# Expert weight loads held behind the first gathered rows, and a cross-attention output product in halves

## The chip, the cores and the metric

The kernel runs on one core of one Trainium2 chip. The metric is the device time of one execution in microseconds (us). The core has five engines that run their own queues: PE (matrix products), DVE (vector work), ACT (activations and copies), POOL, which here issues the indirect transfers, and SP, which issues most plain transfers. All transfers run on the core's 16 DMA engines. PE's granted clock stands in the profile as a share of full speed.

## The reference

Two transformer blocks in float32 on 512 tokens of width 1024. The change touches only the end of the second block: cross attention to a memory of 256 rows, and after it a mixture of 16 experts, of which each token uses two.

```python
x = x + cross_attention(rmsnorm(x, norm_xa_g), rmsnorm(mem, norm_mem_g), xa_wq, xa_wk, xa_wv, xa_wo)
x = x + hierarchical_moe(rmsnorm(x, norm_moe_g), ...)
return rmsnorm(x, norm_final_g)

def hierarchical_moe(h, ...):
    ...                                   # group softmax, best group, top 2 of its 4 experts
    a = jnp.einsum("nd,edf->nef", hf, w_gate)      # 1024 -> 256 per expert
    b = jnp.einsum("nd,edf->nef", hf, w_up)
    u = jax.nn.silu(a) * b * combine[..., None]    # combine: routing weights, zero for experts not chosen
    return jnp.einsum("nef,efd->nd", u, w_down)    # 256 -> 1024
```

## The kernel before

Tokens stand in four tiles of 128 rows (`self.x[t]`, two halves of 512 columns). Products keep float32 precision by splitting each operand into a high and a low part: `wsplit` makes the high part on ACT (a copy) and the low part on DVE (a subtraction), and each product is three matmuls (`mm_as`, lines L380 to L382). So every weight tile costs a load (`wl`, 512 KB), an ACT and a DVE instruction (`ws`, L354 and L357) before PE can use it.

**The end of cross attention.** `cross_out(t)` multiplies the attention output of tile t by `w_xo` in two halves n and adds each to `x` (L1420). `route_unit(t)` then routes the tile: transposes of `x` (L1466), the logits (L1480, L1482), the choice of experts on DVE (L1484 to L1499), the rank of each token within its expert (L1506, L1509), and the normed rows `hr` (L1501), which SP writes to DRAM as `rows_d` (L1502). When tile 3 is through, `slot_ids` (L1551, L1552) gives for each expert the list `ids` of up to 96 rows. `weigh` (L1540 to L1545) puts the routing weights into the same slots: 8 products on PE and 16 small DVE instructions.

**The experts.** `expert(i)` gathers the rows of expert i by an indirect transfer of POOL (`gat`, L1667), transposes them on PE (L1674), splits them (`eh`, L423, L424), multiplies by the gate and up weights (24 matmuls, `wg` from four `wl` tiles), and later multiplies by the down weights (`wed`, four tiles of 256 KB; L1720 for the second half). POOL adds the result into DRAM (`acc_d`, L1726). A pipeline of generators (`pipe`) starts a new expert in each round; expert 16 is one that takes what overflows the 96 slots, and its weights are chosen by a register (L1628).

**The loads.** `fetch_all` is one list of steps, in order of experts: one step for each `wl` tile of the gate and up weights, and one for the four `wed` tiles of an expert, two experts behind. The cross attention takes the first `PF2` steps while it runs; then each round of the expert stage takes `NF` = 4 more. All are issued by SP, in order, and each waits until its buffer is free (the pool `p` holds the `wl` tiles, the pool `u` the `wed` tiles) and until the eighth transfer before it has landed. `rows_d` stands in the same queue, so it is issued between weight loads. With 18 steps, all of the gate and up weights of experts 0 to 3 and the down weights of experts 0 and 1 are asked for during cross attention; expert 4 follows in the first round.

The program's order on each engine is set by a scheduler that runs before the kernel is built; the lists below are taken from the built programs.

Of the kernel before, what the change touches and what calls it, by code (L numbers as in the profile page):

```python
# [22 lines left out]
NT = 4  # L23
# [9 lines left out]
FD, NF = 2, 4  # L33
# [21 lines left out]
CAP = 96  # L55
NX = 2 * S // CAP
HEADS = (slice(0, 64), slice(64, 128))
LAG = (1, 1, 1, 1)
PF0, PF1, PF2 = 2, 1, 18


def f32(ap):
# [3 lines left out]
def fl(t):  # L66
    return t.rearrange("p a b -> p (a b)")
# [111 lines left out]
def run(gen):  # L179
    for _ in gen:  # L180
        pass


def chain(*gens):
    for g in gens:
        yield from g


def pipe(gens, width, newest=False):

    act, gens = [], iter(gens)
    while True:
        if len(act) < width:
            g = next(gens, None)
            if g is not None:
                act.append(g)
        if not act:
            return
        for g in act[::-1] if newest else list(act):
            if next(g, g) is g:  # L200
                act.remove(g)
        yield


def take(gen, n):
    for _ in range(n):
        if next(gen, gen) is gen:
            return
        yield
# [15 lines left out]
class Block:  # L225
# [18 lines left out]
    def open(self, ctx):  # L244
        self.xp = self.sb(ctx, "xp")
        self.wk = self.sb(ctx, "work")
        self.n = N1
        self.nsplit, self.stage = -1, 0
        nc, ins = self.nc, self.ins
        self.x = [self.xt("x") for _ in range(NT)]  # L250
        self.load_x(0, 2)
        nc.sync.dma_start(self.ident, ins["ident"])
        nc.sync.dma_start(self.vec, ins["vec"])
        self.w_lora = [self.load(ins["w_lora"][:, g:g + 2, :], 160) for g in range(0, KD, 2)]
        self.load_x(2, 4)
# [88 lines left out]

    def load(self, src, n=512, tag="r"):
        t = self.pt("wl", F32, tag)[:, :src.shape[1], :n]
        self.nc.sync.dma_start(t, src)
        return t

    def wsplit(self, t, tags="hl"):  # L350

        nc = self.nc
        hi, lo = (self.pt("ws", F32R, g)[:, :t.shape[1], :t.shape[2]] for g in tags)
        nc.scalar.activation(hi, t, AF.Copy)  # L354
        self.nsplit += 1
        eng = nc.gpsimd if self.nsplit % 4 in SP[self.stage] else nc.vector
        eng.tensor_tensor(lo, t, f32(hi), ALU.subtract)  # L357
        return [(hi[:, j], lo[:, j]) for j in range(t.shape[1])]
# [16 lines left out]
    def mm_as(self, ps, ws, act, t, m=128):  # L375
        nt = self.nc.tensor
        sl = slice(t * m, (t + 1) * m)
        for k, (wh, wl) in enumerate(ws):
            ah, al = act[k]
            nt.matmul(ps, ah[:, sl], wh, start=k == 0, stop=False)  # L380
            nt.matmul(ps, ah[:, sl], wl, start=False, stop=False)  # L381
            nt.matmul(ps, al[:, sl], wh, start=False, stop=k == len(ws) - 1)  # L382

    def proj(self, src, act, use, rest=None, ws=None):

# [1026 lines left out]
    def cross_out(self, t, wo, z):  # L1412
        yield
        yield
        a = [(z[:, 0, h * 128:(h + 1) * 128], z[:, 1, h * 128:(h + 1) * 128]) for h in range(4)]
        for n in range(2):
            ps = self.ps("mm")
            self.mm_as(ps, wo[n], a, 0)
            x = self.x[t][:, n]
            self.nc.vector.tensor_tensor(x, x, ps, ALU.add)  # L1420
        yield


# [215 lines left out]
    def fetch_down(self, i):  # L1639

        w = []
        for ed in self.ed[i]:
            for k in range(2):
                w.append(self.ut("wed"))
                self.nc.sync.dma_start(w[-1], ed[:, k])
        self.ed[i] = w
        yield

# [7 lines left out]
    def expert(self, i, add=True, skip=dict(bounds_check=S - 1, oob_is_err=False)):  # L1656

        nc = self.nc

        def lag(n):  # L1660
            for _ in range(LAG[n]):
                yield

        raw = self.ew.pop(i)
        g = fl(self.xt("gat"))[:CAP]

        nc.gpsimd.indirect_dma_start(out=g, out_offset=None, in_=self.rows, **skip,  # L1667
                                     in_offset=bass.IndirectOffsetOnAxis(ap=self.ids[:CAP, i:i + 1], axis=0))
        yield from lag(3)
        a = []  # L1670
        for q in range(2):
            ps = self.ps("tp")[:, :4 * CAP]
            for k in range(4):
                nc.tensor.transpose(ps[:, k * CAP:(k + 1) * CAP], g[:, (4 * q + k) * 128:(4 * q + k + 1) * 128],  # L1674
                                    self.ident[:CAP, :CAP])
            z = self.pt("eh", F32R)
            h, l = (z[:, n, :4 * CAP] for n in range(2))
            self.split_to(h, l, ps)
            a += [(h[:, k * CAP:(k + 1) * CAP], l[:, k * CAP:(k + 1) * CAP]) for k in range(4)]
        self.stage = 6  # L1680
        with ExitStack() as c:

            for ins in self.last_of if i < 2 else ():
                c.enter_context(self.tc.issue_after(ins.ins))
            wg = [w for t in raw for w in self.wsplit(t)]
        yield from lag(0)
        ps = self.ps("mm")[:CAP]
        self.mm_as(ps, wg, a, 0, CAP)
        u = self.at("eu")[:CAP, :256]
        nc.scalar.activation(u, ps[:, :256], AF.Silu)  # L1690
        nc.vector.scalar_tensor_tensor(u, u, self.ws[:CAP, i:i + 1], ps[:, 256:], ALU.mult, ALU.mult)
        yield from lag(1)

        ed = self.ed.pop(i)
        hi, lo = self.pt("wdh", F32R, "r"), self.pt("wdl", F32R, "r")
        for k in range(2):
            self.split_to(hi[:, k], lo[:, k], ed[k])
        wd = [(hi[:, k], lo[:, k]) for k in range(2)]
        tp = self.ps("tp")
        for k in range(2):  # L1700
            nc.tensor.transpose(tp[:, k * CAP:(k + 1) * CAP], u[:, k * 128:(k + 1) * 128], self.ident[:CAP, :CAP])
        z, zf = self.tg("euT", "a", F32R), self.at("euF")
        self.split_to(z[:, :2 * CAP], z[:, 256:256 + 2 * CAP], tp[:, :2 * CAP])
        nc.scalar.copy(zf[:, :2 * CAP], tp[:, :2 * CAP])
        a = [(z[:, k * CAP:(k + 1) * CAP], z[:, 256 + k * CAP:256 + (k + 1) * CAP]) for k in range(2)]
        yield from lag(2)
        if add:
            y = self.kt("ey")[:CAP]
        else:
            oh = self.tg("oh", "u", F32R)[:CAP]  # L1710
            self.onehot(oh, i)
            yh, yl = (self.pt("yl", F32R)[:CAP] for _ in range(2))
            self.last += [(oh, yh), (oh, yl)]
        for n in range(2):
            ps = self.ps("mm")[:CAP]
            if n == 0:
                self.mm_as(ps, wd, a, 0, CAP)
            else:
                for k in range(2):
                    nc.tensor.matmul(ps, zf[:, k * CAP:(k + 1) * CAP], ed[2 + k], start=k == 0, stop=k == 1)  # L1720
            if not add:
                self.split_to(yh[:, n], yl[:, n], ps)
            else:
                nc.scalar.copy(y[:, n], ps)
        if add:
            nc.gpsimd.indirect_dma_start(  # L1726
                out=self.acc, out_offset=bass.IndirectOffsetOnAxis(ap=self.ids[:CAP, i:i + 1], axis=0),
                in_=fl(y), in_offset=None, compute_op=ALU.add)
        yield

    def moe(self, out):
        with ExitStack() as c:
            self.psum(c, "moe", mm=4, tp=3, r=1)
            p = pipe((self.expert(i, i < LAST) for i in range(17)), 16)
            ps, self.last = self.ps("r"), []
            self.route_weights()
            more = chain(self.weigh(self.ws[:CAP, 0:16], ps[:CAP, 0:16], self.rk, self.asg, 16), self.route_more())
            for n, _ in enumerate(p):
                run(take(self.fetches, NF))
                for _ in range(6 if n == 0 else 2):  # L1740
                    next(more, None)
                if n == GB:
                    gb = self.bcast_row(3)
            xs = [self.xt("fx") for _ in range(NT)]
            hs = [self.pt("fh") for _ in range(NT)]
            self.final(out, gb, xs, hs, self.last)
# [100 lines left out]
```

## Time and profile before

| | us |
|---|---|
| median of 3 runs | 1454.07 |
| range of the runs | 1453.44 to 1454.4 |
| the profiled execution, its own time | 1445.03 |
| its span in the trace | 1443.2 |
| PE busy | 1370.2 (95%) |
| DVE busy | 875.6 (61%) |
| ACT busy | 623.8 (43%) |
| POOL busy | 51.3 (4%) |
| mean granted clock of PE | 0.974 |

The profile is of one execution, 9 us shorter than the median of the runs. Its times are counted from the first instruction. Cross attention ends near 1226 us, the routing of the last tile takes until 1240 us, and the expert stage with the final norm fills the rest. The profile also says what each instruction waited for, in brackets behind its row.

### The profile page before, as it was taken

To read this page: it belongs to the slowest core of one execution; us is meant where nothing else is said; L and a number is where in the kernel's file an instruction comes from. 1 tells how busy PE (TensorE), PEld (TensorE's weight loads), DVE (VectorE), ACT (ScalarE), POOL (GpSimd) and SP (SyncE) were. 2 spreads that over 40 slices of the span, in tenths; PEclk is the share of its full clock that TensorE was granted. 3 is DMA by queue.
4 is the path that set the end of the run, shared out by engine and by line. 5 is a ranking of instruction groups with operands and counts; after the bars stand their busy time and mean duration, and the time that the engine had idled before them with its cause. 6 is when DMAs were issued, how large, how long until landed. Compare 5 with 4: busy or idle time off the path is not lost.

```text
span 1443.2 us, 21699 instructions
## 1 busy us (share of the span) xinstructions
PE 1370.2 (95%) x8366; PEld 1080.2 (75%) x8366; DVE 875.6 (61%) x2035; ACT 623.8 (43%) x1143; POOL 51.3 (4%) x45
## 2 busy tenths in 40 slices
PE   5999999998889999999999999999999998699996
PEld 5877776776588888888888887776788897466663
DVE  5347465646775145343367485997456566799875
ACT  5244235533334243232344414444432453487873
POOL 0000000000000000000000000000000000232211
PEclk9999999999899999999999999999999999699998
DMA  5322420121223233232242315222122345799984
GB/s 204 104 79 71 157 75 15 38 91 52 64 84 99 76 117 102 74 117 96 80 146 88 99 29 171 84 62 85 59 92 87 123 169 190 240 311 338 334 286 144
DMA packets 67759, 178.01 MB, mean 123 GB/s; under 512 B 17144, under 2 KB 18552, under 8 KB 67648
## 3 DMA queue, kind: packets, MB, share of 16 engines
q1 hardware_dynamic: 58676, 156.39, 32.7%
q0 software_dynamic: 3584, 10.10, 3.2%
q10 hardware_dynamic: 5388, 10.06, 2.0%
q8 instruction: 68, 1.11, 0.3%
q14 instruction: 43, 0.35, 0.1%
HBM read 163.12 MB, written 15.88 MB: 124 GB/s over the span
## 4 chain that ended last, share of the span: by engine, by line
PE 82%; DVE 10%; DMA 3%; ACT 2%; issue 2%; SPq 0%; DVEq 0%; ACTq 0%
PE mm L371 11%; PE mm L372 11%; PE mm L373 11%; PE mm L380 10%; PE mm L382 10%; PE mm L381 10%; PE q L966 3%; DVE ws L357 2%; PE mm L1720 2%; PE acc L537 1%; PE s L512 1%; PE tp L531 1%; DVE cacc L1112 1%; PE tp L917 1%; PE mm L917 1%
## 5 line engine op out<-in xcount | busy, mean ns | idle before, releaser
L357 DVE TENSOR_TENSOR ws<-wl,ws 128x1024 fp32r<-128x1024 f32 (+2 forms) x238 | 280.7, 1192 | 141.2 <-ACT ws L354 134.6
L354 ACT ACTIVATE ws<-wl 128x1024 fp32r<-128x1024 f32 (+2 forms) x238 | 244.3, 1034 | 176.3 <-PE mm L382 106.5
L371 PE MATMUL mm<-hT,ws 128*128 128x512 f32 (+3 forms) x872 | 314.7, 365 | 1.7 <-ACT qT L565 0.7
L372 PE MATMUL mm<-hT,ws 128*128 128x512 f32 (+3 forms) x872 | 314.4, 363 | 1.1 <-DVE hT L427 1.0
L373 PE MATMUL mm<-hT,ws 128*128 128x512 f32 (+3 forms) x872 | 313.0, 361 | 0.0
L371 PEld LDWEIGHTS mm<-hT,ws 128*128 128x128 f32 (+2 forms) x872 | 162.4, 188 | 30.1 <-ACT qT L565 1.4
L372 PEld LDWEIGHTS mm<-hT,ws 128*128 128x128 f32 (+2 forms) x872 | 163.2, 188 | 27.2 <-DVE hT L427 2.1
L373 PEld LDWEIGHTS mm<-hT,ws 128*128 128x128 f32 (+2 forms) x872 | 163.0, 187 | 24.9 <-DVE ws L357 0.2
L380 PE MATMUL mm<-ws,ff 128*128 128x512 f32 x256 | 100.0, 391 | 0.0
L382 PE MATMUL mm<-ws,ff 128*128 128x512 f32 x256 | 99.7, 389 | 0.0
L381 PE MATMUL mm<-ws,ff 128*128 128x512 f32 x256 | 99.6, 389 | 0.0
L1112 DVE SCALAR_TENSOR_TENSOR cacc<-sig,vec,cacc 128x507 f32<-128x507 f32 (+25 forms) x120 | 86.1, 733 | 1.6
L1067 DVE TENSOR_TENSOR ur<-ur 128x512 f32<-128x512 f32 x32 | 22.1, 692 | 82.3 <-ACT ff L1066 82.3
L380 PE MATMUL mm<-ws,eh 128*96 128x512 f32 x136 | 56.4, 415 | 1.1 <-ACT eh L423 1.1
L1063 ACT ACTIVATE ur<-mm 128x512 f32<-128x512 f32 x32 | 19.0, 594 | 87.1 <-PE mm L373 87.1
L382 PE MATMUL mm<-ws,eh 128*96 128x512 f32 x136 | 55.5, 408 | 0.7 <-DVE eh L424 0.6
L381 PEld LDWEIGHTS mm<-ws,ff 128*128 128x128 f32 x256 | 48.1, 188 | 9.9
L382 PEld LDWEIGHTS mm<-ws,ff 128*128 128x128 f32 x256 | 48.1, 188 | 10.0
L380 PEld LDWEIGHTS mm<-ws,ff 128*128 128x128 f32 x256 | 48.1, 188 | 9.9
L381 PE MATMUL mm<-ws,eh 128*96 128x512 f32 x136 | 54.7, 402 | 0.0
L521 ACT ACTIVATE sp<-sp,mx 128x128 f32<-128x128 f32 (+3 forms) x64 | 35.7, 558 | 30.2 <-DVE mx L519 30.1
L1086 DVE TENSOR_TENSOR f<-f,mm 128x512 f32<-128x512 f32 x24 | 16.4, 685 | 49.2 <-PE mm L382 49.2
(436 smaller groups left out, 2364.1 us busy)
## 6 DMA issues: line engine op xcount, KB each, us to landing
wl<-w_gu SPq DMA_DIRECT2D x68, 512.0 KB
wl<-w_p SPq DMA_DIRECT2D x60, 512.0 KB
wed<-w_ed SPq DMA_DIRECT2D x68, 256.0 KB
wl<-w_up SPq DMA_DIRECT2D x32, 512.0 KB
wl<-w_dn SPq DMA_DIRECT2D x32, 512.0 KB
wl<-w_out SPq DMA_DIRECT2D x16, 512.0 KB
x<-x SPq DMA_DIRECT2D x8, 512.0 KB
gram_d<-gb SPq DMA_DIRECT2D x8, 256.0 KB
```

The source lines that it names most:

```text
L354: nc.scalar.activation(hi, t, AF.Copy)
L357: eng.tensor_tensor(lo, t, f32(hi), ALU.subtract)
L371: nt.matmul(ps, wh[:, c0:c0 + m], ah[:, sl], start=k == 0, stop=False)
L372: nt.matmul(ps, wh[:, c0:c0 + m], al[:, sl], start=False, stop=False)
L373: nt.matmul(ps, wl[:, c0:c0 + m], ah[:, sl], start=False, stop=k == len(ws) - 1)
L380: nt.matmul(ps, ah[:, sl], wh, start=k == 0, stop=False)
L381: nt.matmul(ps, ah[:, sl], wl, start=False, stop=False)
L382: nt.matmul(ps, al[:, sl], wh, start=False, stop=k == len(ws) - 1)
L521: nc.scalar.activation(sps[h][:, :n], sps[h][:, :n], AF.Exp, scale=-1.0, bias=mxs[h][:, 0:1], accum_out=ls[h])
L917: nc.tensor.matmul(ps[a, c], lhs[a, c], rhs(a, c), start=True, stop=True)
L966: nc.tensor.matmul(ps[a], lhs[a], rhs[a], start=n == 0, stop=n == len(terms) - 1)
L1112: nc.vector.scalar_tensor_tensor(acc[:, d:], up[:, 0:S - d], w(30 - d), acc[:, d:], ALU.mult, ALU.add)
```

## The change

1. `PF2` goes from 18 to 13: cross attention asks for the weights of experts 0 to 2 and the down weights of expert 0 only. The 5 steps left out are taken in the first round of the expert stage, with the 4 of that round.
2. The loads of that round get a real wait (`hold`) for the gather of expert 0: they are issued when its rows have landed. SP's queue is in order, so all later loads follow them.
3. `cross_out` of tile 3 yields between its two halves, so that tile 2's routing can come between them.
4. The transposes of expert 1 are put behind the last gate product of expert 0 on PE; two of the four weight tiles of expert 0 may be split before the routing is over.
5. `weigh` moves from the first round to behind the gate products of expert 0, and `route_more` (the overflow plan) starts two rounds later.

```diff
-PF0, PF1, PF2 = 2, 1, 18
+PF0, PF1, PF2 = 2, 1, 13
...
         t = self.pt("wl", F32, tag)[:, :src.shape[1], :n]
-        self.nc.sync.dma_start(t, src)
+        self.hold(self.nc.sync.dma_start(t, src))
         return t
+
+    def hold(self, dma):
+
+        if self.behind is not None:
+            self.tc.add_manual_dep(dma.ins, self.behind.ins.name,
+                                   mybir.DependencyInfo(mybir.DependencyClass.Sync, mybir.DependencyReason.DATA),
+                                   reason="hold")
...
             self.mm_as(ps, wo[n], a, 0)
             x = self.x[t][:, n]
             self.nc.vector.tensor_tensor(x, x, ps, ALU.add)
+            if n == 0 and t == NT - 1:
+                yield
         yield
...
-        nc.gpsimd.indirect_dma_start(out=g, out_offset=None, in_=self.rows, **skip,
+        ga = nc.gpsimd.indirect_dma_start(out=g, out_offset=None, in_=self.rows, **skip,
                                      in_offset=bass.IndirectOffsetOnAxis(ap=self.ids[:CAP, i:i + 1], axis=0))
+        if i == 0:
+            self.behind = ga
         yield from lag(3)
...
-            for k in range(4):
-                nc.tensor.transpose(ps[:, k * CAP:(k + 1) * CAP], g[:, (4 * q + k) * 128:(4 * q + k + 1) * 128],
-                                    self.ident[:CAP, :CAP])
+            with ExitStack() as c:
+                if i == 1:
+                    c.enter_context(self.tc.issue_after(self.last_of[2].ins))
+                for k in range(4):
+                    nc.tensor.transpose(ps[:, k * CAP:(k + 1) * CAP], g[:, (4 * q + k) * 128:(4 * q + k + 1) * 128],
+                                        self.ident[:CAP, :CAP])
...
+            wg = [w for t in raw[:2] for w in self.wsplit(t)] if i == 0 else []
             for ins in self.last_of if i < 2 else ():
                 c.enter_context(self.tc.issue_after(ins.ins))
-            wg = [w for t in raw for w in self.wsplit(t)]
+            wg += [w for t in raw[len(wg) // 2:] for w in self.wsplit(t)]
         yield from lag(0)
         ps = self.ps("mm")[:CAP]
-        self.mm_as(ps, wg, a, 0, CAP)
+        last = self.mm_as(ps, wg, a, 0, CAP)
+        if i == 0:
+            self.last_of.append(last)
+            run(self.weights)
...
-            more = chain(self.weigh(self.ws[:CAP, 0:16], ps[:CAP, 0:16], self.rk, self.asg, 16), self.route_more())
+            self.weights = self.weigh(self.ws[:CAP, 0:16], ps[:CAP, 0:16], self.rk, self.asg, 16)
+            more = self.route_more()
             for n, _ in enumerate(p):
-                run(take(self.fetches, NF))
-                for _ in range(6 if n == 0 else 2):
+                run(take(self.fetches, NF + (5 if n == 0 else 0)))
+                self.behind = None
+                for _ in range(2 if n > 1 else 0):
                     next(more, None)
```

**SP's queue at the end of the routing.** Rows are instructions in program order, with the semaphores they wait for; DMAHW is the landing of one of SP's or ACT's own transfers, DMASW that of one of POOL's. In the program before, from the last load of expert 3 through the rows of tiles 1, 2 and 3:

```order
L347 DMA wl<-w_gu 128x1024 [waits DMAHW7_49,PE_49]
L1502 DMA rows_d<-hr 128x1024 [waits DMAHW0_49,DVE_49]
L1645 DMA wed<-w_ed 128x512 [waits DMAHW1_49,PE_49]
L1645 DMA wed<-w_ed 128x512 [waits DMAHW2_49,PE_49]
...
L1502 DMA rows_d<-hr 128x1024 [waits DMAHW7_49,DVE_49]
L347 DMA wl<-w_gu 128x1024 [waits DVE_49,DMAHW0_49,PE_49,Activation_49]
L1502 DMA rows_d<-hr 128x1024 [waits DMAHW1_49,DVE_49]
L347 DMA wl<-w_gu 128x1024 [waits DMAHW7_49,DMAHW2_49]
```

And with the change, from the rows of tile 1 on:

```order
L1512 DMA rows_d<-hr 128x1024 [waits DMAHW4_49,DVE_49]
L1512 DMA rows_d<-hr 128x1024 [waits DMAHW6_49,DVE_49]
L1512 DMA rows_d<-hr 128x1024 [waits DMAHW0_49,DVE_49]
L347 DMA wl<-w_gu 128x1024 [waits DMASW0_49,DMAHW1_49,PE_49,Activation_49]
L347 DMA wl<-w_gu 128x1024 [waits DMAHW4_49,DMAHW2_49]
L347 DMA wl<-w_gu 128x1024 [waits DMAHW3_49,PE_49]
L347 DMA wl<-w_gu 128x1024 [waits PE_49,Activation_49]
L1655 DMA wed<-w_ed 128x512 [waits DMAHW5_49]
```

The four loads of expert 3, the four `wed` of expert 1 and the first load of expert 4 have gone from ahead of the last rows to behind them, and the first of them waits for POOL's gather (DMASW0). From expert 10 on the order of the loads is the same in both programs but for single `wed` tiles.

**PE at the first experts.** Before, from the last routing product on (L1542 is `weigh`, L1674 the transposes of gathered rows, L380 to L382 the gate products):

```order
L1513 MATMUL r<-oh 96x16
L1542 MATMUL r<-ohw 96x16 x8
...
L1674 MATMUL tp<-ident,gat 128x96 x8
L380 MATMUL mm<-ws,eh 96x512
L381 MATMUL mm<-ws,eh 96x512
L1674 MATMUL tp<-ident,gat 128x96 x4
L382 MATMUL mm<-ws,eh 96x512
```

With the change, where L1689 are the transposes, L387 to L389 the products and L1552 is `weigh`:

```order
L1523 MATMUL r<-oh 96x16
L1689 MATMUL tp<-ident,gat 128x96 x8
L387 MATMUL mm<-ws,eh 96x512
L388 MATMUL mm<-ws,eh 96x512
L389 MATMUL mm<-ws,eh 96x512
...
L1552 MATMUL r<-ohw 96x16 x5
L1689 MATMUL tp<-ident,gat 128x96 x8
```

The 24 gate products of expert 0 now stand in one piece between its transposes and those of expert 1, and `weigh` has come behind them.

**DVE behind the slot ids.** Before, `ide` and the row after the next are `slot_ids`, `ohw` is `weigh`, and `ws` the first split of expert 0:

```order
L1551 TENSOR_SCALAR ide<-r,cst 96x16
L1540 TENSOR_SCALAR ohw<-cst 128x96
L1552 SCALAR_TENSOR_TENSOR cst<-r,ide 96x16
L1541 TENSOR_SCALAR ohw<-cst 128x16
...
L357 TENSOR_TENSOR ws<-wl,ws 128x1024
L1545 COPY cst<-r 96x16
```

With the change:

```order
L1561 TENSOR_SCALAR ide<-r,cst 96x16
L1580 TENSOR_TENSOR cst<-cst 128x8
L1562 SCALAR_TENSOR_TENSOR cst<-r,ide 96x16
...
L364 TENSOR_TENSOR ws<-wl,ws 128x1024 x3
...
L432 TENSOR_TENSOR wdl<-wed,wdh 128x512 x2
L432 TENSOR_TENSOR eh<-tp,eh 128x384 x2
L1550 TENSOR_SCALAR ohw<-cst 128x96
```

Six small instructions stand between the ids and three splits in a row; the 16 instructions of `weigh` come behind the split of the gathered rows.

## Rows read from the trace of the kernel before

**Rows 1.** Busy time by stretch: us, length, PE, PEld, DVE, ACT, POOL, clock, DMA share, GB/s
```profile
1254.00:1264.00 10.00, 10.00 (x44) 6.87 (x43) 6.53 (x28) 6.57 (x10) 0.95 (x1) 0.88 0.82 225
1264.00:1274.00 10.00, 9.94 (x47) 6.33 (x46) 9.97 (x54) 7.75 (x14) 3.02 (x2) 1.00 1.00 318
...
1384.00:1394.00 10.00, 10.00 (x48) 6.62 (x47) 8.17 (x13) 7.48 (x13) 1.41 (x1) 1.00 1.04 363
1394.00:1404.00 10.00, 8.29 (x27) 4.71 (x26) 6.28 (x15) 6.78 (x12) 1.65 (x1) 0.83 0.78 240
```

**Rows 2.** Waits of SP's queue from 1300 to 1400 us: total, times, longest
```profile
SPq L347 <- DMA wl<-w_gu: 28.5, 19, 2.7
```

**Rows 3.** ACT in order of time near the end: start, length, line, tiles, idle before
```profile
1396.18 1.06 ACT L354 ACTIVATE ws<-wl 128x1024 fp32r<-128x1024 f32 x1 [3.10 <-DMA wl<-w_gu]
```

**Rows 4.** The chain of work that ended last, pieces from 1345 us on: start, length
```profile
1345.10 0.66 PE tp L1674 x8
...
1354.61 0.66 PE tp L1674 x8
...
1386.42 9.68 DMA wl<-w_gu
```

**Rows 5.** SP's queue in order of time, 1197 to 1250 us
```profile
1197.92 0.37 SPq L347 DMA_DIRECT2D wl<-w_gu  x1
...
1200.71 6.12 SPq L347 DMA_DIRECT2D wl<-w_gu  x3
...
1215.89 2.24 SPq L1645 DMA_DIRECT2D wed<-w_ed  x4
...
1232.24 0.33 SPq L347 DMA_DIRECT2D wl<-w_gu  x1
```

**Rows 6.** Queues (q1: SP, q0: POOL) in 1204:1210, 1237:1264, 1264:1396: packets, MB, share
```profile
q1 hardware_dynamic: 673, 1.93, 81.2%
...
q1 hardware_dynamic: 2049, 5.82, 69.5%
q0 software_dynamic: 560, 1.59, 22.8%
...
q1 hardware_dynamic: 13343, 35.58, 76.0%
q0 software_dynamic: 2799, 7.72, 26.4%
```

**Rows 7.** All engines in order of time, 1225 to 1241 us: routing of the last tiles
```profile
1226.02 1.03 PE L1466 MATMUL tp<-ident,x 128*128 128x128 f32 x8
...
1229.87 0.24 DVE L1482 SCALAR_TENSOR_TENSOR cst<-mm,nr_o,cst 128x24 f32<-128x24 f32 x1 [1.17 <-PE mm L1480]
...
1233.57 0.15 DVE L331 TENSOR_SCALAR ms<-ssq 128x1 f32<-128x1 f32 x1
...
1240.02 0.16 DVE L1552 SCALAR_TENSOR_TENSOR cst<-r,ide 96x16 int32<-96x16 f32 x1
```

**Rows 8.** All engines in order of time, 1240 to 1254 us: the first gathers
```profile
1240.38 2.87 PE L1542 MATMUL r<-ohw 128*96 128x16 f32 x16 [0.72 <-DVE ohw L1541]
...
1241.15 1.24 POOL L1667 DMA_INDIRECT gat<-rows_d,cst  x1 [461.86 <-DMA wl<-w_gu]
...
1242.46 1.21 DVE L357 TENSOR_TENSOR ws<-wl,ws 128x1024 fp32r<-128x1024 f32 x1
1242.70 4.28 POOL L1667 DMA_INDIRECT gat<-rows_d,cst  x1 [0.31 <-PE r L1542]
...
1244.90 1.21 DVE L357 TENSOR_TENSOR ws<-wl,ws 128x1024 fp32r<-128x1024 f32 x1
...
1249.30 1.54 PE L1674 MATMUL tp<-ident,gat 96*128 96x96 f32 x8 [5.24 <-DMA gat<-rows_d,cst]
...
1253.38 0.90 PE L1674 MATMUL tp<-ident,gat 96*128 96x96 f32 x4 [1.43 <-DMA gat<-rows_d,cst]
```

**Rows 9.** The last accumulate of POOL, 1405 to 1412 us
```profile
DMA to landing us min/median/max: 5.2/5.2/5.2
```

More of the change, by code (lines that the diff above doesn't have):

```diff
@@ L247, in open @@
         self.n = N1
-        self.nsplit, self.stage = -1, 0
+        self.nsplit, self.stage, self.behind = -1, 0, None
         nc, ins = self.nc, self.ins
@@ L381, in mm_as @@
             nt.matmul(ps, ah[:, sl], wl, start=False, stop=False)
-            nt.matmul(ps, al[:, sl], wh, start=False, stop=k == len(ws) - 1)
+            o = nt.matmul(ps, al[:, sl], wh, start=False, stop=k == len(ws) - 1)
+        return o
     def proj(self, src, act, use, rest=None, ws=None):
@@ L1644, in fetch_down @@
                 w.append(self.ut("wed"))
-                self.nc.sync.dma_start(w[-1], ed[:, k])
+                self.hold(self.nc.sync.dma_start(w[-1], ed[:, k]))
         self.ed[i] = w
```

## Prediction

> **What bounds the kernel now.** Busy time alone says PE: 95% of the span. The expert stage has to be read apart, so I began with busy time by stretch [rows 1]. From 1264 to 1394 us PE is busy in full at the full clock, and the DMA engines show a share of 1.00 to 1.04 as well: two resources without room in the same stage. To see which one gives way, look at who waits at the end. SP's queue, from 1300 us on, waits most for earlier loads to land [rows 2], hardly for buffers: it has the next load ready and can't place it. The chain that ended last runs through a load from 1386.42 to 1396.1 us [rows 4], the first gate and up tile of expert 16, and ACT stands idle 3.10 us for it [rows 3]; PE is down to 8.29 of 10 us there [rows 1]. So PE sets the pace of the stage while a stock of early loads lasts, and the stock is used up exactly at its end. An expert is 2.10 + 1.05 = 3.15 MB of weights. The DMA engines' price follows from the queues' totals [rows 6]: SP's 35.58 MB took 76.0% of 132 us, 2.82 us per MB; POOL's 7.72 MB took 26.4%, 4.51 us per MB. The two shares make 1.024, so a sum of such times is divided by 1.024. The weights alone cost 3.15 x 2.82 / 1.024 = 8.7 us per expert; with a gather and an accumulate (7.72 MB over 24 of them, 0.32 MB each) 2.8 us more, 11.5 us. PE works off an expert in 9.5 us: the transposes of two experts in a row start at 1345.10 and 1354.61 [rows 4]. Each expert eats 2 us of stock.
>
> **What the change does, part by part.**
>
> *The routing ends a little earlier.* Tile 2's eight transposes (1.03 us, [rows 7]) now stand ahead of tile 3's second half, so tile 3's `x` is complete about 1.0 us later; but tile 2's work on DVE, from its logits at 1229.87 to the start of tile 3's norm at 1233.57 [rows 7], no longer waits behind tile 2's late transposes, and starts some 2.5 us earlier. Net 1.5 us earlier, between 0 and 2.5. The ids, complete at 1240.18 before [rows 7], come at 1238.7.
>
> *The gather is alone.* Before, POOL starts it at 1241.15 and the transposes start at 1249.30 [rows 8]: 8.15 us, beside loads issued from 1232.24 on [rows 5]. No run of it without loads is in the trace. Bounds: POOL's own 1.24 us plus 0.31 MB at the pace of the stretch 1204 to 1210 (0.4 MB per us, [rows 6]) is 2.0 us; the upper end is the 8.15. The nearest row is the last accumulate, the same 96 rows by the same queue with the engines free, 5.2 us with reading the old sum [rows 9]. I take 4.7. With 0.3 us for POOL to start, the rows land at 1238.7 + 0.3 + 4.7 = 1243.7 (1241.0 to 1247.2), 5.6 us earlier than 1249.30.
>
> *PE at the first experts.* Expert 0's products start 5.6 us earlier; the wait of 1.43 us for the second gather in the middle of them [rows 8] goes, because expert 1's transposes now stand behind all 24. `weigh`, which filled PE's wait (2.87 us at half clock, [rows 8]), comes into busy PE: 1.4 us at full clock, at most 2.9; I take 2. DVE's part of it, 16 small instructions, moves into a stretch where DVE has no room either [rows 1]. If PE still set the end, it would come 5.6 + 1.4 - 2 = 5.0 us earlier, plus the 3.1 us of the last wait if the load were there: 8.
>
> *The loads start later and are more.* This is the costly part. Before, between 1237 and 1396 us SP's queue moved 5.82 + 35.58 = 41.40 MB [rows 6], of which 0.52 MB are the last `rows_d`. Ahead of that stretch it had issued five tiles of 0.524 MB (four of expert 3, one of expert 4) and four of 0.262 MB [rows 5], 3.67 MB, that now wait for the gather. So behind 1243.7 there are 41.40 - 0.52 + 3.67 = 44.55 MB to move before expert 16's first tile is in, and of POOL's 9.31 MB all but the first gather, 9.0 MB. At the prices above: (44.55 x 2.82 + 9.0 x 4.51) / 1.024 = 162.3 us. The early loads, before accumulates begin, go at 2.52 us per MB (81.2% of 6 us for 1.93 MB, [rows 6]); for the first 8 MB that takes off 2.4 us. 1243.7 + 159.9 = 1403.6 us instead of 1396.1: 7.5 us later. The difference can be checked the other way: 6.7 us of later start, 10.1 us for 3.67 MB, less 1.4 us for `rows_d`, 1.4 us for the gather, 4.1 us that the engines lost before (the sum by the same prices for 1237 to 1396 is 155.0 of 159.1 us; in 1254 to 1264 the share is 0.82, [rows 1], because the buffers were full) and 2.4 us for the early pace. Two small ones are left out because they are opposite: the queue has to fill again, and part of the second and third gather is through before the loads start.
>
> *What hides the rest.* The early splits of expert 0 and the smaller load in cross attention cost nothing as long as the gather is later than them; without that cover a split is 1.1 us on ACT [rows 3] and 1.2 us on DVE [rows 8]. The overflow plan starts two rounds later; its cover is that expert 16's loads are last in the queue anyway.
>
> **The sum.** Behind the landing of expert 16's first tile the order is the same in both programs, so the 47.1 us from 1396.1 to 1443.2 stay. The span becomes 1443.2 + 7.5 = 1450.7, the profiled execution 1452.5, and on the median, which lies 9.0 us above that execution, 1454.07 + 7.5 = 1461.6 us. PE would be ready 5 us earlier and gets 7.5 us later what it needs: it will wait several times for loads, in the second half of the stage.
>
> **The rivals.**
>
> *The gather comes late* (chance 0.15). In the trace the second gather stays on POOL for 4.28 us, from 1242.70 until just behind the three splits that DVE starts one after the other from 1242.46 to 1244.90; the first, beside small DVE work, takes 1.24 us [rows 8]. With the change three such splits stand six small instructions behind the ids, where the first gather now is. If POOL loses that race by the splits' length, the rows land up to 3.2 us later, and with them all loads: +10.7 us, 1464.8. It decides if the last `rows_d` lands over half a microsecond behind the ids. Against it: `rows_d` has no loads beside it any more.
>
> The Trainium skill ("SBUF — State Buffer", "Who interferes with whom") says that a DVE instruction with two SBUF inputs and a GpSimd instruction that reads SBUF exclude each other, and that the later of the two waits until the first is through. The split is such an instruction, and the 4.28 us beside 1.24 us agree; by that rule the outcome hangs on which of the two is issued first, and a gather that comes second would give the time of this rival.
>
> *Loads keep up, and PE sets the end: faster* (0.20). Then the 8 us from above count: 1446. PE then asks for expert 16's first tile 5 us before 1393, where its wait began, so the 53.55 MB (44.55 + 9.0) would have to pass from 1243.7 to 1388 us, at 371 GB/s; my sum has 335. The break-even, landing at 1396.1, is 351 GB/s, and a gain of 0.2% begins at 358. For it: 363 GB/s stand in one stretch, 1384 to 1394. Against it: 318 from 1264 to 1274 [rows 1], and 328 over 1264 to 1396 (35.58 + 7.72 MB in 132 us, [rows 6]). The rows alone would give it less than the chance I leave it; the sum runs over 160 us of a shared resource, and an error of 7% in it is enough.
>
> *Both meet* (0.15): the rows land at 1241, and the engines go 2% faster than priced (3.2 us): 7.5 - 2.7 - 3.2 = +1.6 us, 1455.7.
>
> That the wait doesn't take hold is excluded: it stands on the first held load in the built program.
>
> **How the numbers follow.** Forecast as summed, 0.50; late gather 0.15; both meet 0.15; faster 0.20. A difference under 0.2%, 2.9 us, is about what a measurement of this kernel can't tell from none. So slower by more 0.65, within 0.15, faster 0.20. The forecast's own range is 1456 to 1468: the landing of the rows gives -2.7 and +3.5, the price of the DMA engines 2% either way, 3.2 us, and 4.1 us of lost room could come back when `wed` buffers are full. To leave out no more than 2 in 10, the range reaches to 1449 on the side of the gain and to 1467.
>
> **What would show it.** Right: the first held load is issued at 1243 to 1245 and the first transposes of gathered rows run there; no wait of PE between expert 0's products; the DMA share is 1.0 or more from some 1246 to 1402 without the dip at 1254; waits of ACT for `wl` appear several times in the second half of the stage, 1 to 3 us each, instead of once; the last load of the chain lands near 1404. Wrong: no ACT wait for `wl` until the end (the engines moved more than 350 GB/s), or expert 0's transposes still near 1249 (the gather did not gain from being alone), or a span below 1440.

## The result, and the profile after

The changed kernel takes 1460.71 us (median of 19 runs, 1450.96 to 1473.03) where the kernel before, on the same chips, takes 1453.44 (19 runs, 1440.29 to 1457.30). The ratio is 1.0062, with a 95% interval of 1.0041 to 1.0082: slower by 0.6%, some 9 us (the two medians lie 7.3 us apart). The forecast was 1461.6 us and slower.

The two profiled executions already differ by 9 us ahead of everything that was changed, so their times are compared from the slot ids on, which are complete at 1240.18 us before [rows 7] and, by the first row below, at 1249.24 after. From there the kernel before needs 203.0 us to the end of its span of 1443.2, the changed one 212.2 to the end of 1461.4: 9.2 us more.

All engines of the changed kernel in order of time, at the first experts (start, us, engine, line; in brackets the idle time ahead and what ended it). L1562 completes the ids, L1677 is the gather, L1689 the transposes of gathered rows, L361 and L364 split gate and up tiles, L431 and L432 split down tiles (`wdh`, `wdl`) and gathered rows (`eh`), L387 is the first of the three products:

```profile
1249.07 0.17 DVE L1562 SCALAR_TENSOR_TENSOR cst<-r,ide 96x16 int32<-96x16 f32 x1
...
1250.22 2.11 POOL L1677 DMA_INDIRECT gat<-rows_d,cst  x1 [458.29 <-DVE cst L1579]
...
1254.70 0.96 POOL L1677 DMA_INDIRECT gat<-rows_d,cst  x1 [0.30 <-issue]
...
1255.53 1.99 SPq L347 DMA_DIRECT2D wl<-w_gu  x4
1257.58 2.67 SPq L1655 DMA_DIRECT2D wed<-w_ed  x4
...
1255.44 1.54 PE L1689 MATMUL tp<-ident,gat 96*128 96x96 f32 x8 [6.66 <-DMA gat<-rows_d,cst]
1272.30 0.74 PE L387 MATMUL mm<-ws,eh 128*96 128x512 f32 x1 [15.32 <-ACT eh L431]
...
1248.63 2.93 ACT L361 ACTIVATE ws<-wl 128x1024 fp32r<-128x1024 f32 x3
1270.57 1.30 ACT L431 ACTIVATE wdh<-wed 128x512 fp32r<-128x512 f32 x2 [19.01 <-DMA wed<-w_ed]
1271.78 0.85 ACT L431 ACTIVATE eh<-tp 128x384 fp32r<-128x384 f32 x2
...
1271.23 1.37 DVE L432 TENSOR_TENSOR wdl<-wed,wdh 128x512 fp32r<-128x512 f32 x2 [17.33 <-ACT wdh L431]
1272.51 1.01 DVE L432 TENSOR_TENSOR eh<-tp,eh 128x384 fp32r<-128x384 f32 x2
```

The rows are there at 1255.4, 6.2 us behind the ids (9.1 before, [rows 8]), and the held loads are issued with them. But expert 0's products begin only at 1272.3. ACT's queue is in order, and ahead of the split of expert 0's rows stand the splits of expert 1's down tiles. These tiles are among the held loads, so ACT waits 19.0 us for them, DVE 17.3 us behind it, and PE 15.3 us behind both. Before, the same tiles were loaded at 1215.89 [rows 5] and split from 1219.65 on, during cross attention, and expert 0's first product came 1.5 us behind the start of its first transpose, 1249.30 [rows 8] (PE, in the kernel before):

```profile
1250.79 0.74 PE L380 MATMUL mm<-ws,eh 128*96 128x512 f32 x1
```

What the same engines do later, busy time by stretch as in [rows 1], and the split of expert 16's first tile:

```profile
1254.00:1264.00 10.00, 1.54 (x8) 1.25 (x8) 0.00 (x0) 0.00 (x0) 3.28 (x4) 0.50 0.86 247
1264.00:1274.00 10.00, 1.70 (x4) 1.10 (x5) 2.77 (x8) 2.02 (x4) 0.00 (x0) 0.50 1.03 362
...
1384.00:1394.00 10.00, 10.00 (x48) 6.63 (x47) 8.04 (x11) 8.40 (x14) 2.42 (x2) 1.00 1.03 327
...
1404.00:1414.00 10.00, 10.00 (x48) 6.63 (x47) 8.18 (x11) 8.40 (x14) 1.45 (x1) 1.00 1.02 351
```
```profile
1415.94 1.06 ACT L361 ACTIVATE ws<-wl 128x1024 fp32r<-128x1024 f32 x1 [0.80 <-DMA wl<-w_gu]
```

PE loses nearly all of 1254 to 1274, at a granted clock of 0.50, and then runs on without a wait, from 1284 on at full clock. The 3.10 us for which ACT waited for this tile before [rows 3] are down to 0.80. The queues' totals from the release of the loads to that tile, 1255.53 to 1415.9 us (packets, MB, share of the 16 engines' time):

```profile
q1 hardware_dynamic: 16570, 44.64, 78.1%
q0 software_dynamic: 3155, 8.70, 23.8%
```

44.64 MB of loads in 160.4 us: the prediction had 44.55 MB in 159.9 us. So two readings fit the same 9 us. Either the loads set the end, as forecast, and the stall at expert 0 only takes time that PE would have spent waiting for loads later (the loads theory); or the stall is the loss and the loads would have kept up (the stall theory). The experiments tell them apart.

### The profile page after: what moved, and what is told of

Its sections match the earlier page's. It is cut to its first block, busy times and chain, and to the rows that moved or that the text cites. A ratio compares the mean times of both kernels' runs of the same rounds, so it can differ in the third digit from the quotient of the medians.

```text
span 1461.4 us, 21703 instructions
## 1 busy us (share of the span) xinstructions
PE 1380.3 (94%) x8366; PEld 1088.2 (74%) x8366; DVE 877.2 (60%) x2035; ACT 624.5 (43%) x1143; POOL 47.2 (3%) x45
## 4 chain that ended last, share of the span: by engine, by line
PE 82%; DVE 9%; DMA 5%; ACT 2%; issue 1%; SPq 1%; ACTq 0%; DVEq 0%; POOLq 0%
PE mm L378 11%; PE mm L379 11%; PE mm L380 11%; PE mm L387 10%; PE mm L388 10%; PE mm L389 10%; PE q L974 3%; DMA wed<-w_ed 2%; PE mm L1739 2%; PE acc L545 2%; DVE ws L364 1%; PE tp L539 1%; PE s L520 1%; DVE cacc L1120 1%; PE mm L925 1%
## 5 line engine op out<-in xcount | busy, mean ns | idle before, releaser
L364 DVE TENSOR_TENSOR ws<-wl,ws 128x1024 fp32r<-128x1024 f32 (+2 forms) x238 | 281.0, 1192 | 138.6 <-ACT ws L361 133.7
L361 ACT ACTIVATE ws<-wl 128x1024 fp32r<-128x1024 f32 (+2 forms) x238 | 244.5, 1034 | 173.6 <-PE mm L389 109.2
L380 PE MATMUL mm<-hT,ws 128*128 128x512 f32 (+3 forms) x872 | 312.8, 361 | 0.0
L380 PEld LDWEIGHTS mm<-hT,ws 128*128 128x128 f32 (+2 forms) x872 | 162.9, 187 | 24.9 <-DVE ws L364 0.2
L387 PE MATMUL mm<-ws,ff 128*128 128x512 f32 x256 | 100.0, 391 | 0.0
L389 PE MATMUL mm<-ws,ff 128*128 128x512 f32 x256 | 99.7, 389 | 0.0
L387 PE MATMUL mm<-ws,eh 128*96 128x512 f32 x136 | 55.7, 410 | 15.4 <-ACT eh L431 15.3
L389 PEld LDWEIGHTS mm<-ws,ff 128*128 128x128 f32 x256 | 48.1, 188 | 10.0
L387 PEld LDWEIGHTS mm<-ws,ff 128*128 128x128 f32 x256 | 48.1, 188 | 9.8
L389 PE MATMUL mm<-ws,eh 128*96 128x512 f32 x136 | 54.6, 401 | 0.0
```

What stands on the lines that cost most here:

```text
L380: nt.matmul(ps, wl[:, c0:c0 + m], ah[:, sl], start=False, stop=k == len(ws) - 1)
L389: o = nt.matmul(ps, al[:, sl], wh, start=False, stop=k == len(ws) - 1)
```

## The experiments

Each kernel was timed against the kernel before on the same chip; ratios are to that, with 95% intervals. The kernel before had medians of 1451.56 to 1452.38 us there, 1 to 2 us below the 1453.44 from which the first expectations were counted.

**The stall taken away.** `eu` are the gate results, the last thing that ACT and DVE make of an expert's gate and up products.

```diff
-        nc.scalar.activation(u, ps[:, :256], AF.Silu)
-        nc.vector.scalar_tensor_tensor(u, u, self.ws[:CAP, i:i + 1], ps[:, 256:], ALU.mult, ALU.mult)
+        eu = [nc.scalar.activation(u, ps[:, :256], AF.Silu)]
+        eu += [nc.vector.scalar_tensor_tensor(u, u, self.ws[:CAP, i:i + 1], ps[:, 256:], ALU.mult, ALU.mult)]
...
-        for k in range(2):
-            self.split_to(hi[:, k], lo[:, k], ed[k])
+        with ExitStack() as c:
+            for ins in eu if i == 1 else ():
+                c.enter_context(self.tc.issue_after(ins.ins))
+            for k in range(2):
+                self.split_to(hi[:, k], lo[:, k], ed[k])
```

> The changed kernel, with the splits of expert 1's down tiles queued behind expert 1's own gate results on ACT and DVE, so that they no longer stand, waiting for a held load, ahead of the split of expert 0's rows. The order of the loads stays as in the changed kernel up to expert 5. Loads theory: the landing of the last expert's first tile, some 160 us after the first gathered rows, sets the end, and the stall of 15 us at expert 0 cost nothing, since PE would have waited for loads later. Then 1457 to 1461 us (1460.7 with the stall; up to 3 us come back because buffers come free earlier), and waits of ACT for gate and up tiles of 10 us or more in sum appear behind 1300 us. Stall theory: PE sets the end and the 15 us are the loss. Then 1446 to 1449 us, and ACT waits for loads under 4 us in sum. In both the wait of PE between the rows of expert 0 and its first product falls from 15.3 us to under 3.

Measured: 1.0084 (1.0054 to 1.0113), 1465.62 us. The first product, ACT's waits from 1250 us on (total, times, longest) and the split of expert 16's first tile:

```profile
1257.68 1.54 PE L1689 MATMUL tp<-ident,gat 96*128 96x96 f32 x8 [6.60 <-DMA gat<-rows_d,cst]
1259.16 0.74 PE L387 MATMUL mm<-ws,eh 128*96 128x512 f32 x1
```
```profile
ACT wdh L431 <- DMA wed<-w_ed: 24.2, 10, 4.4
ACT ws L361 <- DMA wl<-w_gu: 6.5, 6, 3.7
```
```profile
1257.77 1.76 SPq L347 DMA_DIRECT2D wl<-w_gu  x4
...
1419.12 1.06 ACT L361 ACTIVATE ws<-wl 128x1024 fp32r<-128x1024 f32 x1 [3.71 <-DMA wl<-w_gu]
```

PE starts 1.5 us behind the rows instead of 16.9, and nothing is won: the 15 us come back as 30.7 us of ACT waiting for loads (24.2 of them for down tiles, from 1282.71 on), and the tile lands 161.3 us behind the release, where the changed kernel had 160.4. The stall theory, by which the loads would have kept up, falls. The loads theory gets the mechanism, but the time is 5 us above its range, and what these 5 us are stays open.

**The hold on later loads.** The 5 steps of loads that the change moved are put back: expert 3's tiles and expert 1's down tiles go ahead of the hold again.

```diff
-PF0, PF1, PF2 = 2, 1, 13
+PF0, PF1, PF2 = 2, 1, 18
...
-                run(take(self.fetches, NF + (5 if n == 0 else 0)))
+                run(take(self.fetches, NF))
```

> The changed kernel with 18 steps of loads asked for in cross attention, as before the change, and none extra in the first round: the hold behind the first gathered rows stays, but stands on expert 4's loads, so that 3.67 MB (expert 3's gate and up tiles, expert 1's down tiles) go ahead of it. With these down tiles early, nothing of ACT or DVE waits for a held load ahead of expert 0's products. Loads theory: 3.67 MB at 2.82 us per MB by 1.024 are 10.1 us less behind the gathered rows, so 1460.7 - 10.1 = 1450.6, between 1449 and 1453. Stall theory: as the kernel without the stall, 1446 to 1449.

Measured: 0.9988 (0.9965 to 1.0011), 1451.19 us, as the loads theory had it and above the 1446 to 1449 of the stall theory. From the release, 1254.55, to expert 16's first tile, which is split at 1403.6 without a wait, the loads' queue moved 3.8 MB less than in the changed kernel, in 11 us less (149.0):

```profile
1254.55 3.63 SPq L347 DMA_DIRECT2D wl<-w_gu  x7
...
1403.59 1.05 ACT L361 ACTIVATE ws<-wl 128x1024 fp32r<-128x1024 f32 x1
```
```profile
ACT ws L361 <- DMA wl<-w_gu: 0.6, 2, 0.3
```
```profile
q1 hardware_dynamic: 14984, 40.84, 76.9%
q0 software_dynamic: 3093, 8.52, 25.2%
```

**No hold.** As the kernel without the stall, but with nothing for the loads to wait for:

```diff
-        if i == 0:
-            self.behind = ga
```

> The kernel of e1_no_stall without the hold: 13 steps in cross attention, and the rest of the loads behind the last written rows in SP's queue, with no wait for the gather. Loads theory: the loads start some 8 to 10 us earlier than with the hold, so 1450 to 1453 us, 7 to 9 below e1_no_stall. Stall theory: no difference from e1_no_stall beyond the slower gather, which has loads beside it (up to 3 us later rows), so 0 to 3 us above e1_no_stall.

Measured: 1.0039 (1.0008 to 1.0071), 1460.21 us. It is 0.45% or 6.5 us below the kernel without the stall, a little less than the 7 to 9 expected, with intervals that overlap. The time itself misses the expected 1450 to 1453 by 7 us; nearly 5 of them are those by which the kernel without the stall had already come out above its own range. In the profiles all held loads but the first, which goes still earlier, start 9.4 us earlier against the ids (1239.18 - 1242.34 against 1257.77 - 1251.55), and expert 16's first tile lands 5.9 us earlier (161.7 behind the ids instead of 167.6): with the gather beside them the rows come 10.3 us behind the ids instead of 6.1, and the engines moved 327 GB/s instead of 332.

**The loads as before, with the rest of the change** (18 steps, no hold; the diffs are those of the last two kernels).

> The changed kernel with its loads as before the change: 18 steps in cross attention, none extra in the first round, no hold. What is left of the change is the halves of the last output product, the order of expert 1's transposes, expert 0's two early splits and the later routing weights. Loads theory: the landing of the last expert's first tile is where it was before, so the time is that of the kernel before, 1453.4, within 1.5 us. If these parts lift a limit of PE (stall theory, PE sets the end): 5 to 8 us below the kernel before, 1445 to 1448.

Measured: 0.9979 (0.9954 to 1.0004), 1451.11 us, 0.5 us from the median of the kernel before beside it (1451.56), as the loads theory had it. The halves, the order of the transposes and the later routing weights are worth at most a few us together; whether they gain anything can't be told from this.

**Still fewer loads ahead.** As the kernel without the stall, with 8 steps in cross attention and the order of the down splits kept for expert 0 too:

```diff
-PF0, PF1, PF2 = 2, 1, 13
+PF0, PF1, PF2 = 2, 1, 8
...
-                run(take(self.fetches, NF + (5 if n == 0 else 0)))
+                run(take(self.fetches, NF + (10 if n == 0 else 0)))
```

> The kernel of e1_no_stall with 8 steps asked for in cross attention instead of 13, 14 in the first round, behind the hold (and expert 0's down splits also behind its gate results): 3.15 MB more stand behind the first gathered rows, expert 2's gate and up tiles and expert 0's down tiles. Loads theory: 3.15 MB at 2.82 us per MB by 1.024 are 8.7 us more, so 1465.6 + 8.7 = 1474, between 1471 and 1477, 1.2 to 1.6% above the kernel before, and the last expert's first tile lands 168 to 171 us behind the release instead of 161. Rival: what counts is only that the loads wait for the gather, not how many stand behind it; then 1465 to 1467.

Measured: 1.0117 (1.0075 to 1.0159), 1466.82 us. The ratio is just under the expected 1.2 to 1.6%, but the time is 4 us below the expected range and within the rival's 1465 to 1467, and the interval overlaps that of the kernel without the stall: 0.33% or 4.8 us lie between the two, where 8.7 were expected. The times alone don't decide between the two. The profile, of one execution each, speaks for the loads theory: the tile is split at 1417.54, the loads were released at 1248.75, so 168.8 us lie between, 7.5 more than with 13 steps, for 3.1 MB more (44.48 in the kernel without the stall):

```profile
1248.75 1.76 SPq L347 DMA_DIRECT2D wl<-w_gu  x4
...
1417.54 1.06 ACT L361 ACTIVATE ws<-wl 128x1024 fp32r<-128x1024 f32 x1 [3.64 <-DMA wl<-w_gu]
```
```profile
q1 hardware_dynamic: 17667, 47.58, 78.3%
```

**Fewer bytes, with the stall and without it.** These two complete a square with the changed kernel and the one without the stall. The bytes are taken from behind the hold: for experts 3 to 9 only two of the four down tiles are loaded, and both halves of the down product use these two.

```diff
-        for ed in self.ed[i]:
+        for ed in self.ed[i][:1] if 3 <= i < 10 else self.ed[i]:
             for k in range(2):
                 w.append(self.ut("wed"))
                 self.hold(self.nc.sync.dma_start(w[-1], ed[:, k]))
+        w = (w + w)[:4]
```

> The changed kernel, stall and all, with 3.67 MB of loads left out behind the hold: for the experts 3 to 9 only the first two of the four down tiles are loaded, and the second half of the down product uses them again (so that part of the computation is changed). Loads theory, in its form after the first experiments: the stall and the loads each set the end at nearly the same time in the changed kernel (PE ran from expert 0 to the end with 1.2 us of ACT waits for loads, and the last expert's first tile was split 0.8 us late). Then fewer loads alone give almost nothing: 1458 to 1461 us, 0.3 to 0.6% above the kernel before, ACT's waits for loads behind the stall near 0, and the last expert's first tile landed some 10 us before it is split. Rival: loads alone set the end; then 10 us come off, 1450 to 1452.

> The kernel of e1_no_stall with the same 3.67 MB of loads left out behind the hold (the second half of the down product of the experts 3 to 9 uses the tiles of the first half). Loads theory: 3.67 MB at 2.82 us per MB by 1.024 are 10.1 us; from 1.0084 that leads to 1.0015 of the kernel before, 1453 to 1457 us, and the last expert's first tile lands 149 to 153 us behind the release instead of 161. Rival (something else in the late start costs, such as PE's clock or the changed order on DVE): less than half of it comes off, 1459 or more.

| ratio to the kernel before | all loads | 3.67 MB fewer |
|---|---|---|
| with the stall | 1.0062 (1.0041 to 1.0082) | 1.0058 (1.0034 to 1.0083) |
| without the stall | 1.0084 (1.0054 to 1.0113) | 0.9993 (0.9968 to 1.0018) |

With the stall, fewer loads change nothing (1460.50 us); without it they take off 0.9%, 13 us (1452.62), and the tile is split 148.7 us behind the release without a wait, both just below the expected ranges. First products and ACT's waits, of the kernel with the stall and fewer loads,

```profile
1272.97 0.74 PE L387 MATMUL mm<-ws,eh 128*96 128x512 f32 x1 [13.98 <-ACT eh L431]
```
```profile
ACT wdh L431 <- DMA wed<-w_ed: 17.8, 1, 17.8
ACT ws L361 <- DMA wl<-w_gu: 0.7, 2, 0.3
```

and of the kernel with neither, with the release and the split of the tile:

```profile
1256.07 1.89 SPq L347 DMA_DIRECT2D wl<-w_gu  x4
1257.46 0.74 PE L387 MATMUL mm<-ws,eh 128*96 128x512 f32 x1
...
1404.78 1.06 ACT L361 ACTIVATE ws<-wl 128x1024 fp32r<-128x1024 f32 x1
```
```profile
ACT wdh L431 <- DMA wed<-w_ed: 9.7, 3, 4.3
```

Behind the stall PE runs through: from 1272.97 it takes 187.1 us to the end of the span, 1460.1 (189.1 in the changed kernel). Loads that have more room are worth at most these 2.0 us to it, and nothing that the ratios show. Of the expectation for the first, only the landing can't be seen: the tile is issued 143.7 us behind the release instead of 149.8, 6 us earlier, not 10. With PE late the loads wait for buffers: between 1258 and 1402 SP's loads of `wed` wait 43.5 us for PE, in the changed kernel 14.8.

**PE earlier where the loads just keep up.** In the kernel with the hold on expert 4's loads, DVE worked off the routing weights ahead of the split of expert 0's rows. Here they come behind it:

```diff
+            with self.tc.issue_after(lo.ins), self.tc.issue_after(last.ins):
+                run(self.weights)
...
+                    for ins in self.first if n == 2 else ():
+                        c.enter_context(self.tc.issue_after(ins.ins))
```

(`lo` is DVE's split of expert 0's rows, `last` expert 0's last gate product, `first` that product and DVE's part of its gate results; the second pair of lines stands ahead of `route_more`.)

> The kernel of e2_hold_from_expert4 with the routing weights and the overflow plan behind the split of expert 0's rows on DVE and behind expert 0's gate products on PE. In e2 DVE worked them off ahead of that split: expert 0's first product began 3.7 us behind its first transpose instead of 1.5, and then waited 1.7 us more. In e2 ACT waited 0.6 us for loads in all and PE ran from expert 0 to the end, so the loads theory says that there PE sets the end: the 2.2 + 1.7 us come off, less up to 2 us for the weights' products in busy PE. Then 2 to 4 us below e2, 1448 to 1450, 0.3 to 0.5% under the kernel before, and ACT's waits for loads rise to 1 to 4 us. Rival: e2's loads were just in time, and the time stays at e2's, within 1 us, with ACT's waits for loads up by what PE gained.

Measured: 1.0023 (0.9999 to 1.0046), 1453.70 us: not faster. The 2 to 4 us that the loads theory expected to gain here did not come; the rival, by which loads and PE just met, is nearer, though the time is 2.5 us above the kernel it comes from and not within 1. PE's first product does start 1.5 us behind the first transpose, and all of it is given back to loads:

```profile
ACT wdh L431 <- DMA wed<-w_ed: 11.9, 7, 2.9
ACT ws L361 <- DMA wl<-w_gu: 6.0, 5, 3.8
```
```profile
q0 software_dynamic: 3212, 8.87, 26.3%
```

The tile lands 151.3 us behind the release instead of at most 149.0. In that time POOL's queue moved 8.87 MB, 0.35 more than in the kernel it comes from: a PE that is ahead has the accumulates written earlier, and they pass the engines ahead of the last loads. At 4.48 us per MB (26.3% of 151.3 us for 8.87 MB) that is 1.6 us. This is argued from the rows, not tried.

**The halves alone**, on the kernel before.

> The kernel before with one part of the change alone: the last output product of the cross attention yields between its halves. Forecast of the prediction: the ids come 1.5 us earlier (0 to 2.5), counted from the first gate and up load of the expert stage: 91.0 us behind it where the kernel before shows 92.5. Rival: the 1.0 us that tile 3's second half loses takes it all back, 92.3 to 92.7. In time both say: at most 1 us from the kernel before, 1452.4 to 1454.4, since loads go on setting the end.

Measured: 0.9988 (0.9962 to 1.0014), 1450.50 us: 1.5 us from the median of the kernel before beside it (1451.96), with an interval that includes no difference; both had expected at most 1 us. The ids come 91.6 us behind the first gate and up load (1248.11 - 1156.51, from the start of the load to the start of the last instruction of the ids), between the two forecasts. The other kernels that have the halves show 89.8 to 95.1, so the part can't be told from the spread of single executions.

## Why the prediction came out right, and where it was wrong

**What bounds the stage: right.** PE and the DMA engines both have no room, and the loads' stock decides. From the release to expert 16's first tile the engines moved 334 GB/s in the changed kernel, 332 without the stall, 332 with the hold on expert 4's loads and 336 with 8 steps ahead; the sum had 335. The DMA share stays at 1.01 to 1.05 from 1264 to 1414 in the changed kernel, as the prediction's signs had it.

**The loads start later and are more: right, and the term that carried the forecast.** 160.4 us for 159.9. Taking 3.67 MB from behind the release, in two different ways, leads from 1.0084 to 0.9988 and to 0.9993, 13 to 14 us where 10.1 were priced, with intervals of some 4 us on each ratio; putting 3.1 MB more there gives 7.5 us in the profile and 4.8 in the ratios where 8.7 were priced. From the ids the tile lands 10.7 us later than before (1415.9 - 1249.24 against 1396.1 - 1240.18), where 7.5 + 1.5 = 9.0 were forecast; of the difference of 1.7 us 1.2 are the gather's and 0.5 the loads'.

**The tail unchanged: nearly.** 45.5 us behind the landing instead of 47.1. In the other kernels in which ACT waits for that tile it is 45.5 (the halves alone) to 47.5 (the loads as before), so 1.6 us are within what single executions differ by.

**The closeness of the sum: in part luck.** From the ids to the end 203.0 + 7.5 + 1.5 = 212.0 us were forecast and 212.2 measured, but the tile landed 1.7 us later than forecast and the tail was 1.6 us shorter. And the kernel in which PE does what the prediction describes is the one without the stall: its ratio of 1.0084 is some 12 us, 5 more than forecast. That the changed kernel comes out at the forecast rests on a stall as well that the prediction did not have.

**Routing 1.5 us earlier: not seen.** The ids come 92.3 us behind the first gate and up load, 92.5 before (counted from start to start).

**The gather alone: right in kind, its gain mis-sized.** 6.2 us from the ids to the rows, where 0.3 + 4.7 = 5.0 were forecast. POOL starts it 1.0 us behind the ids, not 0.3; it did so before, too (1241.15 - 1240.18, [rows 7] and [rows 8]), so that this term could have been read ahead. The gather takes 5.2. The rival of the late gather was there in small: the three splits of DVE begin at 1250.05, 0.17 us ahead of POOL's instruction, which took 2.11 us where the third gather, with DVE idle, takes 0.96. That is 1.15 us more, the length of one split, not of three. The Trainium skill ("SBUF — State Buffer", "Who interferes with whom") says that the one that comes later waits for the whole instruction of the other: by that rule one split is what it costs, and this row agrees. The 4.28 us of [rows 8], beside three splits, do not: that is 3.3 us more than 0.96, nearly all three. Why the gather lost to one split here and to three there, no run shows; so the rival's price, taken from the 4.28, was too high for this order.

**PE at the first experts: wrong, and this is the step that failed.** The prediction had PE 5.0 us earlier and named the cover "as long as the gather is later than them" for the early splits. In fact PE's first product came 23.1 us behind the ids (1272.30), 10.6 before (1250.79). What was missed is who waits for the held data: the prediction followed SP's queue behind the hold, but not the queues of ACT and DVE, in which the splits of two held tiles stood ahead of the split of the first rows: a wait for a held load that the sum put at nothing, and that cost PE 15.3 us. The order of DVE shown ahead of the prediction has them, `wdl<-wed,wdh` right ahead of `eh<-tp,eh`.

**"ACT waits for `wl` several times in the second half": wrong for the changed kernel, right in kind without the stall.** Without it ACT waits six times for `wl`, all behind 1390, though only the last is over 1 us; the larger part, 24.2 us, is for down tiles and begins at 1282.71, so loads are short soon behind the release and not only at the end. In the changed kernel the stall gave PE the same lateness that the loads had. Behind it PE needs 189.1 us, and the loads' path from the release leads to the same end within 1 us (the 0.80 of that wait), so each of the two causes alone gives nearly the whole loss, and in the square above removing only one of them shows no gain.

**The rivals.** "Loads keep up" is refuted by the kernel without the stall, which should then have been the faster one. "Both meet" came true in a way that was not meant, later by the stall instead of earlier by a fast gather.

No version tried is shown to beat the kernel before; the lowest ratio is 0.9979 with an interval that ends at 1.0004.

Open are two things: why the kernel without the stall is slower than the changed one in the ratio (its tile lands 0.9 us later, its tail is 1.5 us longer, with POOL's queue at 8.90 MB instead of 8.70), where the intervals overlap; and the loss of the kernel that starts PE earlier, beside the 1.6 us argued above. PE's clock doesn't explain the first up to the landing of the tile: without the stall PE waits for loads early, and its granted clock falls there, but the DMA engines stay busy in full, as in this stretch of the kernel without the stall (columns as in [rows 1]):

```profile
1314.00:1324.00 10.00, 8.70 (x39) 6.28 (x40) 7.91 (x14) 6.70 (x11) 1.50 (x2) 0.83 1.03 338
```

## What to carry to other kernels

When a transfer is made to wait, look up every instruction that reads its data and what stands behind that instruction in its engine's in-order queue; the wait of SP alone tells half. Where the transfer engines are full, as here, the bytes behind the release, by the pace of the stage, give the end, and an earlier start of the other engine is handed back as waits. And a stall that hides the symptom of another bound has to be tested together with it: removing either alone shows no gain.

## What the runs showed of the hardware that was not expected

The runs of the kernel before spread over 17 us (1440.29 to 1457.30), and the profiles show part of such a spread far ahead of the changed part, along with PE's granted clock. Between 300 and 600 us it is 0.98 in one profile (the kernel that starts PE earlier) and 0.92 in another (the halves alone), in columns as in [rows 1]:

```profile
300.00:600.00 300.00, 284.07 (x1903) 231.79 (x1900) 153.78 (x361) 106.97 (x184) 0.53 (x1) 0.98 0.26 84
```
```profile
300.00:600.00 300.00, 286.21 (x1873) 231.56 (x1868) 149.91 (x359) 103.11 (x180) 0.53 (x1) 0.92 0.24 78
```

The first gate and up load is issued at 1144.74 in the first and at 1156.51 in the second, 11.8 us apart. The two profiled executions compared at the start differ in the same way, 0.97 before and 0.93 after in this stretch. Over whole runs time and clock go together: of 23 runs of the kernel before, the fastest (1438.09 us) has a mean granted clock of 0.979, the slowest (1457.69) of 0.961. That the clock is the whole of it was not tried. A difference of a few us between two profiles of such a kernel has to be counted from an event close to the change.
